# The seam between attention and the output projections: last gate products placed between its steps, last head split from PSUM, five heads' outputs loaded into the places of E

## The chip, the cores and the metric

The kernel runs on one core of a Trainium2 chip. The metric is the device time of one execution in microseconds (us). Before the change it is 1768.91 us, the median of three runs (1768.19, 1768.91 and 1770.76).

A core has engines that run side by side, each through its own list of instructions in its own order. PE multiplies matrices, DVE and ACT do elementwise work, POOL here mostly clears small tiles, and SP issues nearly all DMA transfers. They meet through semaphores: an instruction waits until another engine, or a transfer, has counted far enough. While it waits, everything behind it on its engine waits too.

## The reference, cut to what matters

One layer of a decoder, on 1024 tokens of width 1024. The change concerns the end of the attention branch and the start of its projection:

```python
h = rms_norm(x, attn_norm_w)
q, k, v, u, g = split(h @ w_in)                 # g: 2048 columns, 16 blocks of 128
p = softmax(q1 k1 * scale + bias) - lam * softmax(q2 k2 * scale + bias)   # causal, 8 heads
a = rms_norm(p @ v, subln_w) * (1 - lam_init)   # per head, 128 wide
y_a = a.reshape(S, 1024) @ w_proj_attn
c = silu(layer_norm(causal_conv(u_a * sigmoid(u_b)), conv_ln_w, conv_ln_b))
y_b = c @ w_proj_conv
g_a, g_b = split(sigmoid(g + gate_b))
x = x + (g_a * y_a + g_b * y_b) @ w_out
x = x + swiglu(rms_norm(x, ffn_norm_w))
```

## The kernel before, in words

Every float32 product is made of three: both operands are split into a high part (a cast on ACT, `split_hi`, line 120) and a remainder (a subtraction on DVE, `split_lo`, line 125), and `mm3` (lines 152 to 155) adds high times high, high times low and low times high in one PSUM bank. A block of 512 tokens by 128 columns over the 1024 inputs is `gemm_T`: 8 steps of 3, so 24 products of 128x512.

The weights come through a stream, `ws`, that loads two blocks ahead. Its split tiles (`whi`, `wlo`) have three places, so the cast of a later block waits until the products of the block three places before it are done.

The gates. For each of 16 column blocks c, `g_item(c)` makes two halves (`G0` to `G15` below): 24 products into a bank `pg`, a copy with bias on ACT into `sgg`, a store to DRAM in `g_d`. While attention runs, a list `later` holds these and the Q items as filling between attention steps; `plan` says how many pieces each head gets. The last entry of `later`, `["G14", "G15"]`, belongs to no head.

Attention. A loop goes over 8 heads h times 8 blocks i of 128 queries. `scores(h, i)` makes the scores of both softmax halves in banks `sc`; DVE adds the bias and finds the minimum into tiles `E` (four places); ACT takes the exponential (line 1059); DVE joins the two halves (lines 1065 to 1069). In the loop's next turn `turn(h, i)` transposes the joined E on PE (`pT`, line 1088) and splits it into `ph` and `pl`. For each pair of blocks, `weigh(h, b)` multiplies with V (`pW`, 24 products of 128x256 for the last pair), `back` transposes the result (`pB`) and scales it into `an`, `subln` normalises the head, and `subln_T` transposes it (`pS`), scales it into `at` and stores it to DRAM in `a_d`. Everything outside the products that a head needs is put between pieces of G or Q products by hand: `after(ins)` makes what is written in its block stand behind `ins` on its engine.

After the loop (lines 1210 to 1226), the kernel turns, weighs and normalises the last pair of the last head, while the products of G14 and G15 stand behind its `weigh`. Then the pools of attention close, and the tiles `aT_hi` and `aT_lo` of all 8 heads are made from loads of `a_d` in halves of 512 tokens, 16 loads of 256 KB (`early` for heads 0 to 3, `at` for 4 to 7), each followed by its two splits. The first two column blocks of the projection run with the head k as the outer loop, so that they can start on the first head alone (lines 1344 to 1351). The layer norm of the convolution (`ln_chunks`) is spread between the projection's column blocks. PE meets it in its own list at two products `mean`, two `pm` and two `rstd`, and DVE makes the sums for them (`lns`) between other work. A tile scheduler orders what the code leaves open, by its own estimates.

## Time and profile before

| | us |
|---|---|
| runs without the profiler, median of 3 | 1768.91 (1768.19 to 1770.76) |
| the profiled execution, its own time | 1769.82 |
| its span, first to last instruction | 1768.0 |
| PE busy in the span | 1740.1 (98%) |
| DVE busy | 1273.1 (72%) |
| ACT busy | 800.8 (45%) |
| mean granted PE clock | 0.997 |

A profile shows one execution. Times in its views are us from the start of the span. A row of the timeline gives start, busy time, engine, line, operation, out<-in, shape and count; a bracket at its end is idle time of that engine before the row, and what ended it. Busy times of products overlap, since a product's end runs beside the next one's start: the distance between two starts is what a product costs PE. The end of attention lies between 815 and 852 us, and the projection of the heads begins at 851.31.

### The profile page before, as it was taken

The page shows a single profiled execution, that of the slowest core. Times are in us where ns is not written, and L with a number is a line of the kernel's source. Part 1 is how long each engine was busy: PE and PEld are TensorE (multiplying, and loading weights), DVE is VectorE, ACT ScalarE, POOL GpSimd, SP SyncE. Part 2 cuts the span into 40 slices and gives each one's busy share as a digit, 9 for nine tenths or more (in the row PEclk, how much of TensorE's full clock was granted, in tenths as well). Part 3 has the DMA queues.
Part 4 walks back from the last instruction along what each step waited for, and adds up shares of the span by engine and source line. Part 5 has one row for each costly group of instructions (what it writes and reads, how often), then busy time and mean ns, then how long its engine had stood idle before and what let it go on. Part 6 is the DMA issues. An engine that isn't in the chain of part 4 may idle for free.

```text
span 1768.0 us, 25005 instructions
## 1 busy us (share of the span) xinstructions
PE 1740.1 (98%) x8983; PEld 1484.6 (84%) x8983; DVE 1273.1 (72%) x2171; ACT 800.8 (45%) x1883; POOL 19.6 (1%) x92
## 2 busy tenths in 40 slices
PE   6999999999999999999999999999999999999999
PEld 5778898998999998987788888878888888888887
DVE  6598888998898888885677534867667666665544
ACT  5221141557767776754457313633333333333332
POOL 0000000000000000000000000000000000000000
PEclk9999999999999999999999999999999999999999
DMA  6337334235443244341973544224544544697663
GB/s 231 107 125 232 131 111 115 70 104 138 120 141 105 82 125 145 97 147 60 339 261 108 167 166 143 90 90 152 171 159 148 177 153 148 202 357 250 214 214 131
DMA packets 251110, 275.29 MB, mean 156 GB/s; under 512 B 16505, under 2 KB 166050, under 8 KB 250986
## 3 DMA queue, kind: packets, MB, share of 16 engines
q1 hardware_dynamic: 249130, 267.47, 47.0%
q0 software_dynamic: 1280, 4.91, 0.9%
q10 hardware_dynamic: 576, 1.31, 0.3%
q8 instruction: 71, 1.16, 0.3%
q14 instruction: 53, 0.43, 0.1%
HBM read 176.59 MB, written 78.68 MB: 144 GB/s over the span
## 4 chain that ended last, share of the span: by engine, by line
PE 91%; DMA 3%; DVE 2%; ACT 2%; issue 1%; SPq 0%; DVEq 0%; ACTq 0%
PE acc L1611 19%; PE pg L153 14%; PE pg L154 14%; PE pg L155 14%; PE acc L497 12%; PE pg L688 4%; PE sc L1053 2%; PE sc L1052 2%; PE pT L1088 2%; PE wo L154 2%; PE wo L153 2%; PE wo L155 2%; PE pW L155 1%; PE pW L153 1%; PE pW L154 1%
## 5 line engine op out<-in xcount | busy, mean ns | idle before, releaser
L569 DVE SCALAR_TENSOR_TENSOR acc<-u,cw,acc 128x1024 f32<-128x1024 f32 x240 | 306.9, 1279 | 2.9
L153 PE MATMUL pg<-hT_hi,whi 128*128 128x512 f32 x512 | 201.7, 394 | 0.5 <-ACT hT_hi L120 0.2
L154 PE MATMUL pg<-hT_lo,whi 128*128 128x512 f32 x512 | 200.9, 392 | 0.0
L155 PE MATMUL pg<-hT_hi,wlo 128*128 128x512 f32 x512 | 200.7, 392 | 0.0
L120 ACT CAST whi<-wraw 128x1024 fp32r<-128x1024 f32 x101 | 106.1, 1051 | 182.9 <-PE pg L154 99.5
L125 DVE TENSOR_TENSOR wlo<-wraw,whi 128x1024 fp32r<-128x1024 f32 x101 | 123.0, 1219 | 63.3 <-ACT whi L120 59.4
L125 DVE TENSOR_TENSOR wlo<-draw,whi 128x1024 fp32r<-128x1024 f32 x75 | 91.8, 1224 | 89.1 <-ACT whi L120 86.1
L153 PE MATMUL pg<-whi,hT_hi 128*128 128x256 f32 x512 | 146.0, 285 | 0.3 <-ACT jk L756 0.3
L155 PE MATMUL pg<-whi,hT_lo 128*128 128x256 f32 x512 | 145.8, 285 | 0.0
L154 PE MATMUL pg<-wlo,hT_hi 128*128 128x256 f32 x512 | 145.5, 284 | 0.0
L120 ACT CAST whi<-draw 128x1024 fp32r<-128x1024 f32 x75 | 79.1, 1055 | 129.5 <-PE acc L497 122.6
L1059 ACT ACTIVATE E<-E,mn 128x256 f32<-128x256 f32 (+7 forms) x128 | 99.6, 780 | 45.9 <-DVE mn L1054 44.7
L497 PE MATMUL acc<-wlo,whi 128*128 128x512 f32 x308 | 119.8, 389 | 0.0
L497 PE MATMUL acc<-whi,wlo 128*128 128x512 f32 x308 | 119.8, 389 | 0.0
L153 PEld LDWEIGHTS pg<-hT_hi,whi 128*128 128x128 f32 x512 | 96.2, 188 | 20.5 <-ACT sgg L603 0.7
L155 PEld LDWEIGHTS pg<-hT_hi,wlo 128*128 128x128 f32 x512 | 96.2, 188 | 19.1
L154 PEld LDWEIGHTS pg<-hT_lo,whi 128*128 128x128 f32 x512 | 96.2, 188 | 19.0 <-issue 0.6
L153 PEld LDWEIGHTS pg<-whi,hT_hi 128*128 128x128 f32 x512 | 97.7, 191 | 2.2 <-ACT jk L756 1.0
L154 PEld LDWEIGHTS pg<-wlo,hT_hi 128*128 128x128 f32 x512 | 97.7, 191 | 1.3
L155 PEld LDWEIGHTS pg<-whi,hT_lo 128*128 128x128 f32 x512 | 97.7, 191 | 0.4
L1611 PE MATMUL acc<-h_hi,whi 128*128 128x512 f32 x240 | 93.4, 389 | 0.0
L1611 PE MATMUL acc<-h_lo,whi 128*128 128x512 f32 x240 | 93.4, 389 | 0.0
(280 smaller groups left out, 4191.1 us busy)
## 6 DMA issues: line engine op xcount, KB each, us to landing
wraw<-in_w_gate_up_dram SPq DMA_DIRECT2D x44, 512.0 KB, 4.8
wraw<-in_w_in_dram SPq DMA_DIRECT2D x38, 512.0 KB, 4.2
qs<-qs SPq DMA_DIRECT2D x96, 128.0 KB, 2.3
wd<-in_w_down_dram SPq DMA_DIRECT2D x44, 256.0 KB, 3.2
tdT<-wd SPq DMA_DIRECT2D x88, 128.0 KB, 4.5
draw<-sdS SPq DMA_DIRECT2D x44, 256.0 KB, 2.6
draw<-tdT SPq DMA_DIRECT2D x44, 256.0 KB, 4.3
wraw<-in_w_in_dram SPq DMA_DIRECT2D x32, 256.0 KB, 3.4
```

Source lines behind the costliest of these rows:

```text
L120: act.copy(dst, src)
L125: last_lo[0] = dve.tensor_tensor(dst, src, f32(hi), op=ALU.subtract).ins
L153: pe.matmul(o, lh, rh, start=start, stop=False)
L154: pe.matmul(o, lh, rl, start=False, stop=False)
L155: last_mm[0] = pe.matmul(o, ll, rh, start=False, stop=stop).ins
L497: m = pe.matmul(o[s_][i][:], l_[:, ts], r_[:, 512:], start=start and j + y_ == 0, stop=j == n - 1 and y_ == 2, skip_group_check=not start,)
L569: dve.scalar_tensor_tensor(acc[0][:], us[c][:, t : t + S], cw[:, c, t : t + 1], acc[0][:], op0=ALU.mult, op1=ALU.add)
L688: last_mm[0] = pe.matmul(o[:], l_, r_, start=first and n_ == 0, stop=last and n_ == len(terms) - 1).ins
L1052: pe.matmul(o[:, :w], qh[:, qs], k, start=True, stop=False)
L1053: last_mm[0] = pe.matmul(o[:, :w], ql[:, qs], k, start=False, stop=True).ins
L1059: act.activation(e[:, :nk], e[:, :nk], AF.Exp, bias=mn[:, j : j + 1], scale=-1.0, accum_out=l[:, j : j + 1])
L1611: pe.matmul(o[:], a_[x_][:, k, :], b_[y_][:, k, :], start=start and k + x_ + y_ == 0, stop=k == 3 and x_ == 1, skip_group_check=not start,)
```

## The change

The list of fillings is run without its last entry, and the work after the loop is written anew:

- The pools of the convolution and of Q and K close right after the loop, and tiles `aTh` and `aTl` of six heads (`KA` = 0, 1, 2, 3, 4, 7) are opened in their place.
- G14's first half (`g_half(14, 0)`) stands right behind the loop, on PE ahead of the last `turn`. Then come `turn`, a `back`, and `weigh` of the last pair. The second half of G14 follows, with the last `back` in its middle, then the two halves of G15.
- Heads 0 to 4 are loaded from `a_d` in one piece each (512 KB) into the four places of `E` and into the place of the bias tile `tb`, and split whole (128x1024). The loads of heads 5 and 6 stay in halves, behind the closing of the attention pools.
- The last head is no longer stored and loaded: its `pS` is scaled and cast by ACT into `aTh` and its remainder is taken by DVE, both straight from PSUM.
- The first two column blocks of the projection take the heads in the order 0, 1, 2, 3, 4, 7, 5, 6.

```diff
+    def g_half(c, sb, w, amid=None):
+        o = gemm_T(w, hT_hi, hT_lo, sb, amid)
+        sg = wp.tile([P, 512], F32, tag="sg", name=nm("sgg"), bufs=2)
+        act.activation(sg[:], o[:], AF.Identity, bias=pcol("gate_b", c))
+        nc.sync.dma_start(g_d[c][:, sb * 512 : (sb + 1) * 512], sg[:])
...
-    fill = run(it for l_ in later for it in l_)
+    fill = run(it for l_ in later[:-1] for it in l_)
...
-    n = len(steps)
-    turn(*steps[-1])
-    weighs.append((n, steps[-1][:1] + (NT // 2 - 1,)))
-    slot(n, len(late))
-    m = last_mm[0]
-    while backs or sublns:
-        n += 1
-        slot(n, 0)
-    with after(m):
-        for _ in fill:
-            bg.step(2)
+    bg.until(0)
+    qk_ctx.close()
+    cv_ctx.close()
+    yp_ctx = ExitStack()
+    ypa = yp_ctx.enter_context(tc.tile_pool(name="ypa", bufs=1, side="right", reuse_waits="tile"))
+    KA = (0, 1, 2, 3, 4, NKT - 1)
...
+    aT_hi, aT_lo = y_tiles("aT", KA)
...
+    hl, bl = H - 1, NT // 2 - 1
+    with behind(E_.PE, E_.Activation, E_.DVE):
+        wg = ws.next()
+        g_half(14, 0, wg)
+    with after(last_mm[0]):
+        turn(*steps[-1])
+        for h, b, ar in ready(backs, len(steps)):
+            back(h, b, ar)
+        ar = weigh(hl, bl)
+    early = {}
+    for h in KA[:-1]:
+        early[h] = aps.tile([P, S], F32, tag="E" if h < 4 else "tb", name=f"early{h}", bufs=4 if h < 4 else 1)
+        nc.sync.dma_start(early[h][:], a_d[h][:])
+    with after(last_mm[0]):
+        g_half(14, 1, wg, lambda: back(hl, bl, ar))
+    subln(hl)
+    with behind(E_.Activation, E_.DVE):
+        for h in KA[:-1]:
+            split_hi(aT_hi[h][:], early[h][:])
+            split_lo(aT_lo[h][:], early[h][:], aT_hi[h][:])
+    wg = ws.next()
+    with after(last_mm[0]):
+        g_half(15, 0, wg)
+    with after(last_mm[0]):
+        for sb in range(2):
+            cs = slice(sb * 512, (sb + 1) * 512)
+            pt = pm("pS")
+            for i in range(4):
+                pe.transpose(pt[:, i * P : (i + 1) * P], AN[hl][:, 4 * sb + i, :], ident[:])
+            hi = aT_hi[hl][:, cs]
+            act.activation(hi, pt[:], AF.Identity, scale=pcol("subln"))
+            dve.scalar_tensor_tensor(
+                aT_lo[hl][:, cs], pt[:], pcol("subln"), f32(hi), op0=ALU.mult, op1=ALU.subtract
+            )
+        g_half(15, 1, wg)
...
-    for k in range(NKT):
+    for n, k in enumerate(KA + KB):
...
```

The first place is on PE, at the end of the loop. `pT<-ident,E` are the transposes of `turn`, of block 6 of the last head in the first two rows and of block 7 (`E_9102`) after; `pB` and `pW` belong to `back` and `weigh`. Before:

```order
L1088 MATMUL pT_9159<-ident,E_9000 128x128 x4
L1088 MATMUL pT_9166<-ident,E_9000 128x128 x3
L1088 MATMUL pT_9172<-ident,E_9102 128x128 x4
L1088 MATMUL pT_9179<-ident,E_9102 128x128 x4
L1108 MATMUL pB_9186<-ident,ar_9098 128x128 x2
L153 MATMUL pW_9194<-ph_9155,vh_8604 128x256
```

After it, the first and the last rows of the part that is new, with the rows around it (`pg_9195` is the bank of G14's first half):

```order
L1091 MATMUL pT_9166<-ident,E_9000 128x128 x3
L153 MATMUL pg_9195<-hT_hi,whi_8859 128x512
L154 MATMUL pg_9195<-hT_lo,whi_8859 128x512
L155 MATMUL pg_9195<-hT_hi,wlo_8860 128x512
...
L1091 MATMUL pT_9223<-ident,E_9102 128x128 x4
L1091 MATMUL pT_9230<-ident,E_9102 128x128 x4
L1111 MATMUL pB_9237<-ident,ar_9098 128x128 x2
L153 MATMUL pW_9245<-ph_9155,vh_8604 128x256
```

The 24 products of G14's first half now stand between the transposes of block 6 and those of block 7; `pT`, `pB` and `pW` of the last pair still follow one another.

The second place is on ACT, at the same point of the program. `E<-E,mn` is the exponential, `whi<-wraw` the cast of a weight block, `sgg<-pg` the copy of a gate half, `ph<-pT` the cast of the transposed E. Before:

```order
L1059 ACTIVATE E_9102,l_9101<-E_9102,mn_9100 128x1024
L1102 COPY ar_9098<-pW_9079 128x256
L120 CAST whi_9258<-wraw_9256 128x1024
L1059 ACTIVATE E_9112,l_9101<-E_9112,mn_9100 128x1024
L603 ACTIVATE sgg_9152<-pg_9127,pvec 128x512
L120 CAST ph_9155<-pT_9159 128x4x128
L120 CAST ph_9155<-pT_9166 128x3x128
L120 CAST ph_9155<-pT_9172 128x4x128
L120 CAST ph_9155<-pT_9179 128x4x128
```

And after the change:

```order
L1062 ACTIVATE E_9102,l_9101<-E_9102,mn_9100 128x1024
L1105 COPY ar_9098<-pW_9079 128x256
L1062 ACTIVATE E_9112,l_9101<-E_9112,mn_9100 128x1024
L601 ACTIVATE sgg_9152<-pg_9127,pvec 128x512
L120 CAST ph_9155<-pT_9159 128x4x128
L120 CAST ph_9155<-pT_9166 128x3x128
L120 CAST whi_9191<-wraw_9189 128x1024
L601 ACTIVATE sgg_9220<-pg_9195,pvec 128x512
L120 CAST ph_9155<-pT_9223 128x4x128
L120 CAST ph_9155<-pT_9230 128x4x128
```

The cast of the weight block moves from ahead of the last exponential to behind the casts of block 6, and the copy of G14's first half (`sgg_9220`) now stands ahead of the casts of block 7.

The third place is in SP's list of transfers, between the last store of the convolution (`c_d_132`) and the loads of the layer norm (`cT_lo<-c_d`). Before, ten rows from the store of G15's first half on:

```order
L604 DMA g_d_148<-sgg_9349 128x512
L1248 DMA early_0_9406<-a_d_109 128x512
L1248 DMA early_1_9410<-a_d_109 128x512
L1248 DMA early_0_9414<-a_d_110 128x512
L1248 DMA early_1_9418<-a_d_110 128x512
L1248 DMA early_0_9422<-a_d_111 128x512
L1248 DMA early_1_9426<-a_d_111 128x512
L1248 DMA early_0_9430<-a_d_112 128x512
L1248 DMA early_1_9434<-a_d_112 128x512
L1248 DMA at_0_9438<-a_d_113 128x512
```

After the change, from the store `c_d_132` on:

```order
L573 DMA c_d_132<-acc_7505 128x1024
L1252 DMA early_9272<-a_d_109 128x1024
L1252 DMA early_9280<-a_d_113 128x1024
L1252 DMA early_9274<-a_d_110 128x1024
L602 DMA g_d_146<-sgg_9152 128x512
L1252 DMA early_9276<-a_d_111 128x1024
L298 DMA wraw_9471<-in_w_proj_attn_dram 128x8x128
L602 DMA g_d_147<-sgg_9220 128x512
L1252 DMA early_9278<-a_d_112 128x1024
L602 DMA g_d_147<-sgg_9315 128x512
L298 DMA wraw_9477<-in_w_proj_attn_dram 128x8x128
L602 DMA g_d_148<-sgg_9370 128x512
```

The loads of heads 0 to 4 stand ahead of the stores of G14 and G15 now, where before all 16 halves stood behind the store of G15's first half.

More of the change, by code (lines that the diff above doesn't have):

```diff
@@ L366, in kt @@
     def kt(m, k):
[L367 removed]
+        return m[k] if isinstance(m, dict) else m[:, k, :]
     def gemm_T(w, mhi, mlo, sb, amid=None):
@@ L600, in g_item @@
         for sb in range(2):
-            o = gemm_T(w, hT_hi, hT_lo, sb)
-            sg = wp.tile([P, 512], F32, tag="sg", name=nm("sgg"), bufs=2)
-            act.activation(sg[:], o[:], AF.Identity, bias=pcol("gate_b", c))
-            nc.sync.dma_start(g_d[c][:, sb * 512 : (sb + 1) * 512], sg[:])
+            g_half(c, sb, w)
             yield
@@ L1209 @@
         due -= int(due + 1e-6)
-    n = len(steps)
-    turn(*steps[-1])
-    weighs.append((n, steps[-1][:1] + (NT // 2 - 1,)))
-    slot(n, len(late))
-    m = last_mm[0]
-    while backs or sublns:
-        n += 1
-        slot(n, 0)
-    with after(m):
-        for _ in fill:
-            bg.step(2)
-    inatt[0] = False
+    assert next(fill, None) is None and not late
     bg.until(0)
-    del pms[1:]
-    at_ctx.close()
     qk_ctx.close()
@@ new lines, with behind @@
+    E_ = mybir.EngineType
+    def behind(*engines):
+        st = ExitStack()
+        for e_ in engines:
+            st.enter_context(after(last_of(e_)))
+        return st
+    hl, bl = H - 1, NT // 2 - 1
[7 more added lines that the diff above has]
+        ar = weigh(hl, bl)
+    assert not backs and not weighs and not sublns
@@ L1241 @@
-    for h in range(H):
+    KB = tuple(k for k in range(NKT) if k not in KA)
+    for d_, more_ in zip((aT_hi, aT_lo), y_tiles("aT", KB)):
+        d_.update(more_)
+    for h in KB:
         for sb in range(2):
             cs = slice(sb * 512, (sb + 1) * 512)
-            if h < 4:
-                at = bp.tile([P, 512], F32, tag=("s", "sq", "z", "csg")[h], name=f"early{h}_{sb}", bufs=2)[:]
-            else:
-                at = bp.tile([P, 512], F32, tag="ya", name=f"at{h}_{sb}", bufs=4)[:]
+            at = bp.tile([P, 512], F32, tag="ya", name=f"at{h}_{sb}", bufs=4)[:]
```

24 lines of the change are left out of this document (14 added, 10 removed).

## The prediction

> **What bounds the kernel now.** I read the page first (span, slices, the chain), then PE's timeline at the end of attention, then the other engines there, then the stages after it.
>
> ```profile
> span 1768.0 us, 25005 instructions
> ...
> PE   6999999999999999999999999999999999999999
> ...
> PE 91%; DMA 3%; DVE 2%; ACT 2%; issue 1%; SPq 0%; DVEq 0%; ACTq 0%
> ```
>
> PE is the bound: 91% of the chain that ended last is PE's own work. A change pays only where PE waits or runs slowly. PE's timeline has four kinds of rows at the seam that tell how much of this there is:
>
> ```profile
> 815.66 0.92 PE L1088 MATMUL pT<-ident,E 128*128 128x128 f32 x7
> 819.74 1.94 PE L1088 MATMUL pT<-ident,E 128*128 128x128 f32 x8 [3.15 <-DVE E L1068]
> 821.47 0.63 PE L1108 MATMUL pB<-ident,ar 128*128 128x128 f32 x2
> 822.22 0.58 PE L153 MATMUL pW<-ph,vh 128*128 128x256 f32 x1
> ...
> 826.55 0.28 PE L153 MATMUL pW<-ph,vh 128*128 128x256 f32 x1
> ...
> 826.91 0.39 PE L153 MATMUL pg<-hT_hi,whi 128*128 128x512 f32 x1
> ...
> 849.64 0.39 PE L155 MATMUL pg<-hT_hi,wlo 128*128 128x512 f32 x1
> 851.31 1.09 PE L153 MATMUL pg<-aTh,whi 128*128 128x512 f32 x3 [1.28 <-ACT aTh L120]
> ```
>
> The brackets show two waits: 3.15 us for the last joined E, and 1.28 us for the first head's cast. Between them something else is slow: from 819.74 to 826.91 PE needs 7.17 us for 8 transposes, 2 more and 24 `pW`. The windows tell why (columns: stretch, length, then busy time of PE, PEld, DVE, ACT, POOL, the granted clock, DMA share, GB/s):
>
> ```profile
> 820.00:822.00 2.00, 2.00 (x10) 1.70 (x8) 1.18 (x3) 0.87 (x2) 0.20 (x1) 0.50 0.82 271
> ...
> 824.00:826.00 2.00, 2.00 (x11) 2.00 (x11) 0.00 (x0) 0.00 (x0) 0.00 (x0) 0.50 0.00 0
> 826.00:828.00 2.00, 2.00 (x14) 1.83 (x13) 0.00 (x0) 0.37 (x1) 0.00 (x0) 0.96 0.00 0
> ```
>
> The granted clock is 0.50 from 820 until about 826: the long wait is followed by a stretch at half speed.
>
> **The sum.** First what the work costs at full clock. A transpose is 0.11 us (the `pS` row below, 8 in 0.88). A `pW` is 0.12 (826.55 to 826.91 is three of them). A gate product: from 826.91 to 849.64 lie 95 steps, 2 `pB` and 8 `pS`, so (22.73 - 10 x 0.11) / 95 = 0.2277 us.
>
> ```profile
> 841.63 0.88 PE pS L1129 x8
> ```
>
> From 815.66 to 851.31 are 35.65 us. The work in it: 27 transposes (15 `pT`, 4 `pB`, 8 `pS`) 2.97, 24 `pW` 2.88, 96 gate products 21.86, together 27.71. So 7.94 us are lost: 3.15 and 1.28 in the two waits, 7.17 - 3.98 = 3.19 in the slow stretch (3.98 is 10 transposes and 24 `pW`), and 0.3 in hops. The change makes the same products, so only these 7.94 us, and what it adds, are at stake.
>
> **Part 1: G14's first half ahead of the last transposes.** It is 24 x 0.2277 = 5.46 us of work that needs nothing from the last head. PE starts it at 815.66 + 0.77 = 816.43 and ends its issue at 821.89. The joined E is there earlier than that:
>
> ```profile
> 815.63 1.05 ACT L120 CAST whi<-wraw 128x1024 fp32r<-128x1024 f32 x1 [0.79 <-PE pg L154]
> 816.58 1.15 ACT L1059 ACTIVATE E<-E,mn 128x1024 f32<-128x1024 f32 x1
> ...
> 820.86 0.59 ACT L120 CAST ph<-pT 128x512 fp32r<-128x512 f32 x1 [1.62 <-PE pT L1088]
> ...
> 816.71 1.23 DVE L125 TENSOR_TENSOR wlo<-wraw,whi 128x1024 fp32r<-128x1024 f32 x1 [1.01 <-ACT whi L120]
> ...
> 818.30 1.28 DVE L1068 SCALAR_TENSOR_TENSOR E<-E,rl,E 128x1024 f32<-128x1024 f32 x1
> ...
> 821.48 0.69 DVE L125 TENSOR_TENSOR pl<-pT,ph 128x512 fp32r<-128x512 f32 x1 [0.82 <-ACT ph L120]
> ```
>
> Even in the old order E is complete at 819.58; now the weight cast (1.05) no longer stands ahead of the exponential, so about 818.7. The 3.15 us are covered with 3 us to spare, and with them goes what I take for the cause of the half clock, another 3.19. If the cover failed, both would come back.
>
> **What is late next.** `pT` and `pB` of the last pair take 1.10 us (821.89 to 822.99), then `pW` needs the first four blocks of `ph` and `pl`. In ACT's new order the copy of G14's first half stands ahead of those casts. A gate product's row is 0.39 long and the last starts at 821.66, so the copy starts near 822.1. Copy 0.69 (row below), cast 0.59, subtraction 0.69 follow one another, so `pW` starts at 824.1: a **new wait of 1.1 us**. Bounds: 0.8, had ACT taken the cast right behind the first four transposes; 1.4, what lay there before (822.22 - 819.74 - 1.10, at half clock).
>
> ```profile
> L603 ACT ACTIVATE sgg<-pg,pvec 128x512 f32<-128x512 f32 x4 | 2.8, 688 | 1.3 <-PE pg L155 1.3
> ```
>
> From there PE is fed: `pW` 2.88, G14's second half with `pB` 5.69 (the copy `ar` has 21 products of time), G15 and `pS` 11.81. The projection starts at 824.1 + 20.4 = **844.5 instead of 851.3**.
>
> **Part 2: heads 0 to 4 in E's places.** Before, their first load is asked for at 845.76 and PE waits for it:
>
> ```profile
> 845.76 4.12 SPq L1248 DMA_DIRECT2D early<-a_d  x8
> ...
> early<-a_d SPq DMA_DIRECT2D x8, 256.0 KB, 5.4
> ...
> 834.06 0.17 DVE L646 TENSOR_SCALAR v<-ssa 128x8 f32<-128x8 f32 x1 [11.04 <-ACT jk L1117]
> ...
> 835.56 1.22 DVE L1122 TENSOR_TENSOR an<-an,r 128x1024 f32<-128x1024 f32 x1
> ```
>
> Now the last of the five is asked for when E's last transpose is done, near 823, and ACT casts them behind the norm of the last head. G14 ends at 832.7; a weight cast (1.05), the copy (0.69) and a square (0.6) stand on ACT, then 2.72 us of small steps and `an` (834.06 to 836.78): `an` at 837.8. Transfers of 256 KB landed in 5.4 us with the queues full; twice the size has 12 us here. Costs: ACT 5 x 1.05 = 5.3, DVE 5 x 1.22 = 6.1 (the 128x1024 rows above), so DVE is done at 843.9. The projection needs head 0 at 844.5 (ready 839.0) and head 4 only 13 products later, at 847.5. G15 hides all this; without that cover DVE's 6.1 would be on the path. So the 1.28 goes, and 0.25 with it that the first three products lose after it (851.31 to 852.24 for 0.68).
>
> **Part 3: the last head from PSUM.** The store, two loads and their landing disappear. ACT scales and casts at once, as `at<-pS` did. The remainder from PSUM with a scale is not in this place before; its nearest row is the same form for K:
>
> ```profile
> L781 DVE SCALAR_TENSOR_TENSOR klo<-pQ,pvec,ks x3: 743/744/750, 703.1 to 768.5; 128x512 fp32r<-128x512 f32 x3
> ```
>
> Two of 0.74 behind 843.9 end at 845.4; the first product that waits for them is the 17th, at 848.1. Nothing on the path; at twice the price, 846.9, still nothing. Heads 5 and 6 are asked for behind the first `cT_lo` load, which waits for the last product on hT_lo (844.3), and are needed 72 products later, at 860.9.
>
> **Total.** 35.65 + 0.25 before, 27.71 + 1.1 after (0.1 of hops in it): 7.0 to 7.1 us less. Against the profiled execution 1769.82 - 7.05 = 1762.8. The median was 0.9 below that execution; the half-clock stretch that I remove may vary from run to run and be part of this, so I carry only half of it: **1762.4**. Behind 851 PE has no wait over 0.15 us until 1176, so a shift there reaches the end, unless PE meets something that has not moved with it.
>
> **The rule of the skill.** The clock first in rows: besides the stretch above, one other wait is followed by 0.50, and one is not.
>
> ```profile
> 1176.58 0.50 PE L1611 MATMUL acc<-T2h,whi 128*128 128x512 f32 x1 [2.42 <-ACT whi L120]
> ...
> 1178.00:1180.00 2.00, 2.00 (x5) 1.63 (x6) 1.22 (x1) 0.96 (x1) 0.00 (x0) 0.50 0.82 228
> ...
> 850.00:852.00 2.00, 0.72 (x4) 0.40 (x3) 0.71 (x2) 1.32 (x3) 0.00 (x0) 1.00 0.93 332
> ```
>
> So 2.42 us were enough once, 1.28 were not. The Trainium skill, "TensorE: Matmul & The Clock Gate", section "Why this matters for your kernels", puts the bound at gaps over about 3 us; the row at 1178 speaks against so late a bound. Its section "Part 4: PE-mode transpose" adds that transposes don't count as busy PE in the same way. By the first rule the new wait of 1.1 us costs no clock; by the second, 1.1 us of transposes and 1.1 of wait lie together.
>
> **Rivals.** (a) *The clock still drops.* Transposes and the new wait make 2.2 us without dense products, near the 2.42 that sufficed. One stretch like that at 1178 (about 3.4 us at half speed) costs 1.7: 1764.1. Against it: 1.28 did not suffice, and busy transposes are not idle. 12%.
>
> (b) *The layer norm gets in the way.* PE's list meets the second `pm` 276 rows behind the projection's start, where it was 305: 29 x 0.2277 = 6.6 us earlier, relative to that start. Before:
>
> ```profile
> 860.00:870.00 10.00, 10.00 (x44) 7.93 (x43) 7.93 (x13) 4.28 (x8) 0.00 (x0) 1.00 1.05 405
> ...
> 920.19 0.69 DVE L1280 TENSOR_TENSOR lns<-lns,lnsq 128x512 f32<-128x512 f32 x1 [2.24 <-ACT lnsq L1277]
> ...
> 923.26 0.79 PE pm L1286 x8
> ...
> L120 ACT CAST aTh<-early 128x512 fp32r<-128x512 f32 x8 | 4.5, 618 | 5.4 <-DMA early<-a_d 5.3
> ```
>
> DVE's sum ended at 920.88, 2.4 us ahead of PE. If the norm's work keeps its distance to the start, PE waits 6.6 - 2.4 = 4.2: 1766.6. Against it: 12 subtractions of half heads leave DVE's full stretch there (12 x 0.6 = 7.2 us), and 12 casts of 0.62 leave ACT's. 13%, some of it smaller.
>
> (c) *Slower: the layer norm does not move at all.* The DMA share is 1.05 at 860 to 870; were the norm bound by transfers, its sum would still end at 920.9, while PE comes to the second `pm` at 844.5 + 276 x 0.2277 = 907.3. The wait is 13.6, the time 1762.4 + 13.6 = 1776.0. It decides from 914.4 on, where the wait eats the 7. Against it: its first load waits for the last product on hT_lo, which moves, and 10 of the 16 halves now load at 816 to 828. 6%.
>
> (d) *The filling doesn't fill.* G14's first half waits for its bank or weights, and the old wait stays under another name, with the slow stretch, and only the end's 1.28 + 0.25 are gained: 1769.8 - 1.5 = 1768.3. The weights were split long before, and the bank's last copy was of G13's first half. 7%.
>
> **How the numbers follow.** Forecast 62%, within 1760.2 to 1764.6: the low end is 1762.8 less the 0.9 and less 1.7, should the slow stretch at 1178 fall away by chance; the high end adds the wait's bound and small waits. The range goes up to (b), 1760.2 to 1766.6. A measurement of this kernel can tell about 0.2%, 3.5 us, from no change. Faster by more: the forecast, (a) and the small part of (b), 78%. Within: the rest of (b), and (d), 15%. Slower 7%.
>
> **What would show it.** In the new profile: no bracket at the transposes of block 7; a clock of 1.00 through 816 to 845; a bracket near 1 us at the first `pW`; the first `aTh` product near 844.5 with no bracket; no bracket at `mean`, `pm` or `rstd`. A new wait at any of the last three, or 0.50 behind `pW`, makes the prediction wrong by the prices above.

## The result, and the profile after

| | before | changed |
|---|---|---|
| runs beside each other, median | 1770.8 us (6 runs, 1768.19 to 1772.96) | 1764.17 us (6 runs, 1761.77 to 1765.22) |
| ratio | | 0.9964, 95% interval 0.9953 to 0.9976 |
| the profiled execution and its span | 1769.82, 1768.0 | 1765.22, 1763.4 |

The changed kernel is faster by 0.36% (0.24% to 0.47%), 6.4 us of 1770.8 by that ratio. The forecast was 1762.4 within 1760.2 to 1766.6. The page of the changed kernel, its span and the shares of the chain that ended last:

```profile
span 1763.4 us, 24974 instructions
...
PE 90%; DMA 3%; DVE 3%; ACT 2%; issue 1%; SPq 0%; ACTq 0%; DVEq 0%
```

PE still bounds the kernel. PE's timeline at the seam, in the order of the rows shown before:

```profile
816.21 0.92 PE L1091 MATMUL pT<-ident,E 128*128 128x128 f32 x7
...
822.46 1.04 PE L1091 MATMUL pT<-ident,E 128*128 128x128 f32 x8
823.34 0.38 PE L1111 MATMUL pB<-ident,ar 128*128 128x128 f32 x2
824.61 0.39 PE L153 MATMUL pW<-ph,vh 128*128 128x256 f32 x1 [0.89 <-DVE pl L125]
...
845.08 0.39 PE L153 MATMUL pg<-aTh,whi 128*128 128x512 f32 x1
```

The bracket of 3.15 at the transposes of block 7 is gone, and eight of them take 1.04 instead of 1.94. The first product on `aTh` has no bracket. One new bracket stands at the first `pW`. The windows (stretch, length, busy time of PE, PEld, DVE, ACT and POOL, granted clock, DMA share, GB/s) where the clock stood at 0.50 before:

```profile
820.00:822.00 2.00, 2.00 (x10) 1.66 (x9) 1.49 (x2) 0.00 (x0) 0.00 (x0) 1.00 0.95 337
...
824.00:826.00 2.00, 1.39 (x11) 1.40 (x12) 1.15 (x2) 1.55 (x7) 0.00 (x0) 1.00 1.14 334
```

From the first transposes of block 6 to the first `aTh` product there were 35.65 us before; now there are 845.08 - 816.21 = 28.87. So the seam is 6.78 shorter, but the span of this execution only 4.6. PE's waits in the stage behind the seam, 850 to 1000 us (engine, line, what it waited for, us, times, longest), have two new rows:

```profile
PE pg L153 <- ACT cT_hi L120: 0.9, 1, 0.9
PE rstd L1336 <- DVE lnz L1339: 0.7, 1, 0.7
```

Both are waits for the layer norm.

### The profile page after: what moved, and what is told of

Read it like the earlier page. It is cut to its first block, busy times and chain, and to the rows that moved or that the text cites. A ratio compares the mean times of both kernels' runs of the same rounds, so it can differ in the third digit from the quotient of the medians.

```text
span 1763.4 us, 24974 instructions
## 1 busy us (share of the span) xinstructions
PE 1737.2 (99%) x8983; PEld 1481.3 (84%) x8983; DVE 1272.2 (72%) x2166; ACT 799.0 (45%) x1876; POOL 19.6 (1%) x92
## 4 chain that ended last, share of the span: by engine, by line
PE 90%; DMA 3%; DVE 3%; ACT 2%; issue 1%; SPq 0%; ACTq 0%; DVEq 0%
PE acc L1656 21%; PE pg L153 12%; PE pg L154 12%; PE pg L155 12%; PE acc L497 12%; PE pg L691 4%; PE sc L1056 2%; PE sc L1055 2%; PE pT L1091 2%; PE wo L153 2%; PE wo L155 2%; PE wo L154 2%; DMA ya_d<-gt 1%; PE pW L155 1%; DMA gt<-g_d 1%
```

## How the runs are compared

Single executions of one kernel differ by 2.6 to 6.3 us, once by 8.6, and most of the edits below are worth 1 to 7. What repeats far better is the length of a stage in the profiles, between two rows of PE's timeline. The marks are the starts of: the transposes of block 6 (`pT`, x7), the first product on `aTh`, the first on `cT_hi`, the first on `wo`, and the first on `T2h` in the feed-forward. Each number is the difference of two such starts; the first and the last column are what lies ahead of block 6 and behind `T2h`. All in us:

| kernel | ahead | seam | aTh to cT_hi | cT_hi to wo | wo to T2h | behind | span |
|---|---|---|---|---|---|---|---|
| before | 815.66 | 35.65 | 92.01 | 87.04 | 146.22 | 591.42 | 1768.0 |
| changed | 816.21 | 28.87 | 93.07 | 88.44 | 146.22 | 590.59 | 1763.4 |
| changed, again | 815.40 | 28.87 | 93.04 | 87.04 | 146.25 | 590.20 | 1760.8 |
| filler only | 817.98 | 38.06 | 94.59 | 87.04 | 146.20 | 591.43 | 1775.3 |
| filler only, loads first | 816.11 | 31.05 | 94.97 | 87.04 | 146.22 | 592.01 | 1767.4 |
| no filler | 816.00 | 33.96 | 91.73 | 87.04 | 146.22 | 590.05 | 1765.0 |
| short filler | 816.39 | 30.54 | 91.72 | 87.03 | 146.25 | 589.07 | 1761.0 |
| late loads | 814.89 | 29.02 | 92.45 | 87.04 | 146.22 | 589.78 | 1759.4 |
| last head by store | 815.46 | 28.86 | 93.00 | 87.04 | 146.20 | 590.04 | 1760.6 |
| turn inside the filler | 816.29 | 27.82 | 92.12 | 87.03 | 146.23 | 591.01 | 1760.5 |
| five gate tiles | 815.39 | 28.86 | 92.62 | 90.01 | 146.30 | 590.32 | 1763.5 |
| gates behind the norm | 816.11 | 28.87 | 91.95 | 87.04 | 146.21 | 590.62 | 1760.8 |
| turn inside, gates behind | 814.33 | 27.82 | 92.52 | 87.04 | 146.27 | 590.62 | 1758.6 |

What is to be seen: the seam of the changed kernel is 28.86 or 28.87 in five profiles, its own two and those of three kernels whose edits leave PE's seam as it is. The stage ahead (814.3 to 818.0) and the stage behind (589.1 to 592.0) differ by up to 3.7 us without any edit that reaches them. That is the noise of single executions, and a verdict below rests on the stage that an edit touches. Part of the noise goes with the clock. Every profile has the wait of 2.42 us at the first product on `T2h`; in 7 of the 13 a stretch at granted clock 0.50 follows it, in 6 it does not (below), and the last column averages 591.0 with that stretch and 590.0 without.

## The experiments

### The parts one by one

The change has three parts: the filler (G14's first half ahead of the last turn), the early loads (heads 0 to 4 into E's places), and the last head straight from PSUM. First the filler alone, with nothing else of the change:

```diff
-    with behind(E_.Activation, E_.DVE):
-        for h in KA[:-1]:
-            split_hi(aT_hi[h][:], early[h][:])
...
-            hi = aT_hi[hl][:, cs]
-            act.activation(hi, pt[:], AF.Identity, scale=pcol("subln"))
+        subln_T(hl)
...
-    for h in KB:
+    for h in range(H):
```

> Only the filler of the change is kept: the first half of gate product 14 stands ahead of the last turn (and the second half and product 15 behind it, as in the change). Heads 0 to 4 are loaded again into the layer norm's buffers behind the attention, the last head goes through its store and load, and the output products run in the order of the heads. Theory of the prediction (the filler alone takes away the 3.15 us wait and the half-clock stretch; the loads alone take away 1.28 + 0.25): no bracket of 3 us at the transposes of block 7, granted clock 1.00 through the seam, and the waits of 1.28 and 0.25 us on the splits at the first output products are back. The time stands about 1.5 us above the changed kernel: 1765.7 against 1764.2. Rival (what the loads gain at the seam is given back in the layer norm, because the layer norm does not get earlier by as much as the products do): the two waits that the changed kernel has in the layer norm (0.74 us ahead of the rstd transposes, 0.85 us at the first product on cT_hi) shrink here by about as much as the start of the output products is later, and the time is that of the changed kernel within 0.4 us.

Measured: 1776.39 us (5 runs, 1774.43 to 1777.04) beside 1769.63 before; ratio 1.0038, interval 1.0025 to 1.005. Both theories missed: the filler alone makes the kernel slower. PE's row at the first `aTh` product:

```profile
856.04 1.22 PE L153 MATMUL pg<-aTh,whi 128*128 128x512 f32 x2 [9.04 <-ACT aTh L120]
```

The wait is not 1.28 but 9.04 us. The old wait at block 7 did go (the seam has no other bracket than 0.89 at `pW`), so the filler did its work there and uncovered something else. SP's timeline of this run shows it:

```profile
846.40 0.32 SPq L1135 DMA_DIRECT2D a_d<-at  x1
846.81 0.38 SPq L1289 DMA_DIRECT2D cT_lo<-c_d  x1
...
848.78 0.38 SPq L602 DMA_DIRECT2D g_d<-sgg  x1
849.20 0.43 SPq L1289 DMA_DIRECT2D cT_lo<-c_d  x1
849.67 5.35 SPq L1271 DMA_DIRECT2D early<-a_d  x8
```

The loads of heads 0 to 3 leave at 849.67, behind the last head's store, four loads of the layer norm and the last gate store. Before, they left at 845.76, and G15 ran on for 4 us more. Here PE has nothing left from 847.0 on, 2.7 us ahead of them. The products moved ahead of the last turn had covered this round trip.

Then the late loads and the last head by store, each one part undone from the changed kernel:

```diff
-    KA = (0, 1, 2, 3, 4, NKT - 1)
+    KA = (NKT - 1,)
...
-    early = {}
-    for h in KA[:-1]:
-        early[h] = aps.tile([P, S], F32, tag="E" if h < 4 else "tb", ...)
-        nc.sync.dma_start(early[h][:], a_d[h][:])
```

> The changed kernel without the early loads: heads 0 to 4 are loaded behind the attention into the layer norm's buffers, as before; the filler stays ahead of the last turn, the last head goes straight from PSUM and is the first that the output products take. Theory, after the run with the filler alone (the part of gate products 14 and 15 that is moved ahead of the last turn used to cover the round trip of heads 0 to 4; with it gone from there, the loads stand behind the last gate store in SP's queue and PE waits for them): the 12 products on the last head cover 2.7 of the 9.0 us, so a wait of about 6.3 us stands behind them, with a half-clock stretch behind it, and the time is 1771 to 1774 us. Rival (the 9.0 us came from the last head's store and load, not from heads 0 to 4): no wait over 1.5 us, 1764 to 1766.

Measured: 1763.59 us (5 runs, 1761.32 to 1766.86) beside 1769.21 before; ratio 0.9965, interval 0.9953 to 0.9977. The theory missed, and the rival held in its waits: none at the heads, a seam of 29.02 (the time is 0.4 us under its range). SP's timeline tells what differs from the run with the filler alone:

```profile
838.34 0.32 SPq L602 DMA_DIRECT2D g_d<-sgg  x1
838.75 2.79 SPq L1287 DMA_DIRECT2D early<-a_d  x6
845.41 0.32 SPq L602 DMA_DIRECT2D g_d<-sgg  x1
```

Six of the same eight loads into the same kind of buffers leave from 838.75 on, 11 us earlier (7.8 us earlier counted from the transposes of block 6). The last head's store is gone from SP's list, and the scheduler put them ahead of the last gate store. That the missing store is the reason was not tested apart from the other differences of the two runs.

```diff
-            hi = aT_hi[hl][:, cs]
-            act.activation(hi, pt[:], AF.Identity, scale=pcol("subln"))
-            dve.scalar_tensor_tensor(
-                aT_lo[hl][:, cs], pt[:], pcol("subln"), f32(hi), op0=ALU.mult, op1=ALU.subtract
-            )
+        subln_T(hl)
```

> The changed kernel with the last head's outputs stored and loaded again, as before, instead of split straight from PSUM; the filler stays ahead of the last turn and heads 0 to 4 still come early into E's places; heads 5, 6 and 7 are loaded behind the attention. Theory of the prediction (the straight split is worth nothing on the path, since five heads' products, 13.6 us, stand ahead of it): no wait of PE at the first products on aTh nor between the heads, and the time is the changed kernel's within 0.4 us, 1763 to 1764.5. Rival, after the run with the filler alone (the last head's store stands in SP's queue ahead of loads that are needed soon): heads 5 and 6 come late, PE waits 1 us or more between the heads, and the time is over 1765.

Measured: 1763.27 us (6 runs, 1761.85 to 1767.38) beside 1769.53; ratio 0.997, interval 0.9958 to 0.9981; seam 28.86, no wait between the heads. As the theory said. So with the filler, either of the two other parts is enough, and the second adds nothing that shows.

The cause was still argued from the order of issues, with several things changed at once. The next run changes only the issues in the kernel with the filler alone: the last head's two stores go by ACT's queue, and the loads stand ahead of the last gate store and of the layer norm's loads (`ld3` is the last load of head 3; each `add_manual_dep` orders two transfers within SP's list):

```diff
-            nc.sync.dma_start(a_d[h][:, sb * 512 : (sb + 1) * 512], at[:])
+            (nc.scalar if h == H - 1 else nc.sync).dma_start(a_d[h][:, sb * 512 : (sb + 1) * 512], at[:])
...
-            nc.sync.dma_start(cc[c], c_d[c][:, cs])
+            cl_ = nc.sync.dma_start(cc[c], c_d[c][:, cs]).ins
+            tc.add_manual_dep(cl_, ld3.name, ...)
...
+    tc.add_manual_dep(g_last, ld3.name, ...)
```

> The run with the filler alone, with nothing changed but the order of DMA issues: the last head's two stores go out by ACT's queue instead of SP's, and SP issues the loads of heads 0 to 4 ahead of the last gate store and of the loads of the layer norm's inputs (which wait for the last gate product to free their place). Theory (the 9.0 us wait and the slow clock behind it came from the order in SP's queue: the loads stood behind the last head's store, the first load into the layer norm's place and the last gate store): the loads are issued at about 842 instead of 849.7 us, PE's wait at the first product on aTh falls from 9.0 to under 1.5 us, and the time from 1776.4 to 1764 to 1766. Rival (the loads wait for the memory of the attention's tiles, or the round trip itself is too long): the wait stays over 4 us and the time over 1769.

Measured: 1769.44 us (11 runs, 1766.13 to 1771.7) beside 1769.53; ratio 1.0, interval 0.9991 to 1.0009. From the timelines of SP, ACT and PE:

```profile
839.97 9.51 SPq L1271 DMA_DIRECT2D early<-a_d  x8
...
845.92 0.69 ACT L601 ACTIVATE sgg<-pg,pvec 128x512 f32<-128x512 f32 x1
846.50 2.17 ACT L120 CAST aTh<-early 128x512 fp32r<-128x512 f32 x4
...
847.16 1.66 PE L153 MATMUL pg<-aTh,whi 128*128 128x512 f32 x4 [2.03 <-ACT aTh L120]
```

The issues alone take 7.0 of the 9.0 us (seam 38.06 to 31.05): it was the queue. But the expected 1764 to 1766 is missed by 3 to 5 us. The data are there now; the casts of head 0 stand behind the last head's scaling, a weight cast and the last gate copy in ACT's list and begin at 846.50, while PE is done at 845.1. A half-clock stretch follows the 2.03 us wait (below), and the stage up to `cT_hi` is 94.97, 1.9 more than in the changed kernel. In the changed kernel the five casts are done by 841.3, so PE finds heads 0 to 4 split.

### Without the filler

```diff
+    wg = ws.next()
     with behind(E_.PE, E_.Activation, E_.DVE):
-        wg = ws.next()
-        g_half(14, 0, wg)
-    with after(last_mm[0]):
         turn(*steps[-1])
...
+    with after(last_mm[0]):
+        g_half(14, 0, wg)
     with after(last_mm[0]):
         g_half(14, 1, wg, lambda: back(hl, bl, ar))
```

> All of the change but the filler: both halves of gate product 14 stand behind the last weighing. Theory of the prediction: the wait at the transposes of block 7 is back at 2.3 to 3.2 us, and the half-clock stretch of 3.4 us behind it too (3.2 us of PE time), so that only the 1.5 us at the first output products are gained: 1769.3 us against 1770.8 before and 1764.2 of the change. Rival (the half-clock stretch was not due to this wait, or a wait shorter than 3 us does not bring it): the wait is there and the granted clock stays at 1.00: 1766.1 us. Second rival (the layer norm limits the time as soon as the loads are early): the 1.5 us do not show in the time, 1770.8.

Measured: 1766.75 us (11 runs, 1764.67 to 1768.7) beside 1769.63; ratio 0.9986, interval 0.9977 to 0.9995. PE, ACT and DVE at the seam:

```profile
820.08 1.94 PE L1091 MATMUL pT<-ident,E 128*128 128x128 f32 x8 [3.15 <-DVE E L1071]
...
815.97 1.05 ACT L120 CAST whi<-wraw 128x1024 fp32r<-128x1024 f32 x1 [0.79 <-PE pg L154]
816.92 1.15 ACT L1062 ACTIVATE E<-E,mn 128x1024 f32<-128x1024 f32 x1
...
818.64 1.28 DVE L1071 SCALAR_TENSOR_TENSOR E<-E,rl,E 128x1024 f32<-128x1024 f32 x1
```

and the windows behind the wait:

```profile
820.00:822.00 2.00, 1.92 (x9) 1.95 (x10) 1.18 (x3) 0.59 (x1) 0.00 (x0) 0.50 0.72 232
824.00:826.00 2.00, 2.00 (x12) 2.00 (x11) 0.00 (x0) 0.00 (x0) 0.00 (x0) 0.54 0.89 365
826.00:828.00 2.00, 2.00 (x15) 1.83 (x14) 0.00 (x0) 0.37 (x1) 0.00 (x0) 1.00 0.04 16
```

The theory held in mechanism: wait and half clock are both back, unchanged. The seam is 33.96, 1.69 shorter than before, and the stage behind it 0.28 shorter; 1.28 and 0.25 were expected. The run keeps both the early loads and the last head from PSUM, so it does not tell these two apart. The seam is 5.09 longer than in the changed kernel: that is what the filler is worth once the loads are out of the way. The median lies 2.9 us under before where 1.5 was expected; the interval (0.9 to 4.1 us) holds both.

### How long the filler must be

```diff
-        g_half(14, 0, wg)
+        og = pg()
+        g_ks(og, range(0, 2))
     with after(last_mm[0]):
         turn(*steps[-1])
...
+    with after(last_mm[0]):
+        g_ks(og, range(2, 8))
```

Each step of `g_ks` is 3 products.

> The changed kernel with only 6 of the 24 products of the first half of gate product 14 ahead of the last turn; the other 18 and their copy stand behind the weighing. 6 products take 1.36 us of the 3.15 us, so a wait of about 1.8 us is left at the transposes of block 7. Theory (the granted clock falls with any such wait that is long against its window of 3.4 us; 2.4 us were enough further down in this kernel): a half-clock stretch of 3.4 us follows the 1.8 us wait, and the seam is 1.8 + 3.2 less 0.9 us longer than the changed kernel's, 4 us in all: 1767 to 1768. Rival (1.8 us is too short for it): the granted clock stays at 1.00, the seam is 1 to 2 us longer, 1764.5 to 1765.5.

Measured: 1765.56 us (9 runs, 1762.98 to 1768.58) beside 1769.53; ratio 0.9979, interval 0.9969 to 0.9988. PE's rows and the windows around them:

```profile
816.39 0.93 PE L1091 MATMUL pT<-ident,E 128*128 128x128 f32 x7
...
819.63 1.17 PE L1091 MATMUL pT<-ident,E 128*128 128x128 f32 x8 [0.92 <-DVE E L1071]
820.63 0.41 PE L1111 MATMUL pB<-ident,ar 128*128 128x128 f32 x2
822.33 0.39 PE L153 MATMUL pW<-ph,vh 128*128 128x256 f32 x1 [1.30 <-DVE pl L125]
```

```profile
818.00:820.00 2.00, 1.08 (x8) 0.63 (x6) 1.97 (x4) 2.00 (x4) 0.00 (x0) 1.00 1.14 309
820.00:822.00 2.00, 1.04 (x9) 0.64 (x7) 2.00 (x4) 1.79 (x7) 0.00 (x0) 1.00 0.85 337
```

The seam is 30.54, 1.67 longer than the changed kernel's, so the rival held in size. But the question on a wait of 1.8 us stays open: the wait came out at 0.92, since the weight cast moved behind the exponential here as in the changed kernel, and E was joined earlier. What the run does show: two waits of 0.92 and 1.30, with only 1.4 us of transposes between them, left the clock at 1.00 in this execution.

### The new wait at the weighing

```diff
-        g_half(14, 0, wg)
+        og = pg()
+        g_ks(og, range(0, 4))
     with after(last_mm[0]):
         turn(*steps[-1])
+    with behind(E_.PE, E_.Activation):
+        g_ks(og, range(4, 8))
...
+    with after(last_mm[0]):
         for h, b, ar in ready(backs, len(steps)):
```

> The changed kernel with the last turn put in the middle of the filler: 12 products of gate product 14, then block 7's transposes, then the other 12 products and their copy, then the weighing. Theory (the 0.89 us wait at the first weighing product comes from the copies ph and pl standing behind the copy of the gate product, with nothing left on PE to cover them): that wait goes, the seam from the first transposes of block 6 to the first product on aTh takes 28.0 us instead of 28.87, and the time is 0.9 us less than the changed kernel's, 1763.3. Rival (the layer norm behind the seam sets the end of the stage, so an earlier seam is waited out there): the wait goes, the two waits in the layer norm (0.74 and 0.85 us) grow by 0.9 together, and the time stays at 1764.2. Third: 12 products are too short to cover block 7's softmax chain, and a wait of about 2.8 us less 2 times 2.6 stands at the transposes instead: nothing gained.

Measured: 1762.52 us (5 runs, 1761.51 to 1764.1) beside 1769.63; ratio 0.9963, interval 0.9951 to 0.9975. PE's rows:

```profile
816.29 0.93 PE L1091 MATMUL pT<-ident,E 128*128 128x128 f32 x7
...
819.83 1.04 PE L1091 MATMUL pT<-ident,E 128*128 128x128 f32 x8
823.47 0.38 PE L1111 MATMUL pB<-ident,ar 128*128 128x128 f32 x2
823.61 0.36 PE L153 MATMUL pW<-ph,vh 128*128 128x256 f32 x1
```

No bracket is left: 12 products cover E's chain, the other 12 cover the casts and subtractions `ph` and `pl`. The seam is 27.82, 1.05 shorter than the changed kernel's (0.9 expected). So the wait at `pW` came from a copy and a split with nothing beside them on PE. In the time the step does not show above the noise: 0.9963 beside 0.9964.

### What the layer norm takes back

> The changed kernel itself once more, so that it stands on the same chip beside the runs sent with it. Theory (its time hangs on how late the layer norm's casts are, and these hang on how long single stores and loads of the gate tiles take): 0.9964 of before again, 1763 to 1765 us, with single executions spread over 3 us or more; its profile shows waits of 0.5 to 2.5 us in all at the first products on cT_hi and the rstd transposes, not the same ones in the same sizes. Rival (these two waits are fixed): 0.74 and 0.85 us again.

Measured: 1763.41 us (5 runs, 1762.57 to 1767.03) beside 1769.21; ratio 0.9968, interval 0.9956 to 0.998. The time and the spread came as the theory said, and PE's waits from 850 to 1000 us are not the same ones. But it placed them at `cT_hi` and `rstd`, and there it missed.

```profile
PE pg L153 <- DVE gt L1383: 1.0, 1, 1.0
```

Neither `rstd` nor `cT_hi` waits in this execution; the first projection's banks wait 1.02 us for DVE at 868.12 instead. The last cast to `cT_hi` begins at 959.84 in the first execution and at 956.04 in the second. Part of the reason is in SP's and ACT's timelines. Here the first execution, the one with the wait:

```profile
942.73 0.32 SPq L1384 DMA_DIRECT2D ya_d<-gt  x1
945.61 0.32 SPq L1375 DMA_DIRECT2D gt<-g_d  x1
...
948.40 0.63 ACT L1376 ACTIVATE gt<-gt 128x512 f32<-128x512 f32 x1 [2.03 <-DMA gt<-g_d]
948.94 0.81 ACT L1340 ACTIVATE lnz<-lnz,pvec 128x512 f32<-128x512 f32 x1
...
955.25 0.64 ACT L1376 ACTIVATE gt<-gt 128x512 f32<-128x512 f32 x1 [1.63 <-DMA gt<-g_d]
```

A gate tile is free for the next load only when its last use is stored to `ya_d`. The sigmoids `gt` of the second projection's fourth and fifth gates stand in ACT's list ahead of the layer norm's last two pairs of chunks (`lnz`, then the casts), and wait for their loads. In the second execution the same two sigmoids begin at 944.69 and 951.47, 3.7 and 3.8 us earlier, while PE's first `cT_hi` product is only 0.84 us earlier. But 3.0 of the 3.8 us are there already at a cast ahead of both (938.51 beside 935.48). The lag grew before, from 0.5 us at the sigmoid of 892.02 to 3.2 at that of 919.57, which waited 2.81 us for its load where its counterpart waited 1.70. So these two sigmoids are the end of the chain and not the whole of it, and that the time of single stores and loads decides whether PE notices is read from these rows; no run tests it.

Two tries at this chain. One gate tile more:

```diff
-        g = bp.tile([P, 512], F32, tag="gt", name=nm("gt"), bufs=4)
+        g = bp.tile([P, 512], F32, tag="gt", name=nm("gt"), bufs=5)
```

> The changed kernel with five gate tiles gt instead of four, so that a gate load waits for the store of ya_d of the fifth last use, not of the fourth last. Theory (the layer norm is late because its casts stand in ACT's queue behind sigmoids that wait for gate loads, and those for stores): ACT's waits on gate loads between 846 and 970 us fall from 49 us in all to under 40, the two waits of 0.74 and 0.85 us at the layer norm shrink, and the time is 0.8 to 2.0 us less than the changed kernel's: 1762.2 to 1763.4. Rival (the layer norm is late because of its own chain of sums on DVE and squares on ACT, whose start did not move by as much as the products did): the waits on gate loads change, the two waits on PE stay at 0.7 to 0.9 us, and the time stays within 0.3 us of 1764.2.

Measured: 1766.73 us (11 runs, 1762.62 to 1771.23) beside 1769.63; ratio 0.9986, interval 0.9977 to 0.9996. A miss, and rather slower than the changed kernel: the stage from `cT_hi` to `wo` is 90.01, with a wait of 2.5 us for `cT_hi`. A fifth tile does not make ACT wait less for gates (26.5 us from 846 to 965 beside 26.0 in the changed kernel's first profile; the 49 us that the expectation starts from are not found there). The run refutes the number of tiles as the remedy, not the queue as the cause; what made it slower was not followed further.

The other try leaves the tiles and moves the two sigmoids behind the layer norm's last cast:

```diff
-        act.activation(g[:], g[:], AF.Sigmoid)
+        sig = act.activation(g[:], g[:], AF.Sigmoid).ins
+        if ins is not None:
+            tc.add_manual_dep(sig, ins.name, ...)
...
-                g = gated(g_d[NKT + c], cs)
+                g = gated(g_d[NKT + c], cs, ln_end[0] if sb else None)
```

> The changed kernel with two instructions of ACT placed elsewhere: the sigmoids of the fourth and fifth gate of the second projection (needed by the products of its second half only) stand behind the layer norm's last cast instead of ahead of its last two pairs of chunks. Theory (ACT waits there for gate loads that wait for a store or for a product, with the layer norm's last casts behind them in its queue): the two idle stretches of ACT ahead of these sigmoids (2.03 and 1.63 us in the changed kernel's profile) no longer stand ahead of a layer norm cast, the last cast to cT_hi ends some 3.5 us earlier, the wait of 0.85 us and the 0.56 us of slow spacing at the first product on it are gone, and the time is 1.0 to 1.4 us less than the changed kernel's in the same batch, with a smaller spread. The wait of 0.74 us at the rstd transposes stays, since the gates ahead of it are not moved. Rival (the casts are late from DVE's side): the wait stays at 0.5 us or more, and the time within 0.4 us of the changed kernel's.

Measured: 1763.36 us (7 runs, 1761.05 to 1767.39) beside 1769.21; ratio 0.9968, interval 0.9957 to 0.998. ACT's timeline at the end of the layer norm:

```profile
952.90 0.61 ACT L120 CAST cT_hi<-lnz 128x512 fp32r<-128x512 f32 x1
953.82 0.62 ACT L120 CAST cT_hi<-lnz 128x512 fp32r<-128x512 f32 x1 [0.32 <-DVE lnz L1344]
954.35 1.15 ACT L1379 ACTIVATE gt<-gt 128x512 f32<-128x512 f32 x2
```

The last cast begins at 953.82, 6 us ahead of the changed kernel's first profile (959.84) and 2.2 ahead of its second (956.04). This profile has no PE wait at all from 850 to 1000; the one at `rstd`, which was expected to stay, is absent too. The stages behind the seam are 91.95 and 87.04, together the shortest with the whole filler. In the medians nothing shows: 1763.36 beside 1763.41 in the same batch, and the spread is not smaller. So the expected 1.0 to 1.4 us is missed. That the edit brings the cast forward is shown; that it takes a wait from PE is not, since the second profile without the edit has none at `cT_hi` either.

> Both edits together on the changed kernel: the last turn in the middle of the filler, and the two sigmoids behind the layer norm. Theory: the 0.89 us wait at the weighing and the 0.85 us wait at cT_hi are both gone; 1.0 us less than the kernel with the two sigmoids moved alone, about 2.2 us less than the changed kernel, 1761 to 1762. Rival (what is gained ahead of the layer norm is waited out in it): the time of the kernel with the sigmoids moved alone, within 0.4 us.

Measured: 1763.42 us (5 runs, 1760.35 to 1765.0) beside 1769.21; ratio 0.9962, interval 0.995 to 0.9974. The expected 1761 to 1762 is missed, and the rival's number came: the time is that of the kernel with the sigmoids moved alone. In the profile, however, the seam is 27.82 again and the two norm waits are absent. It has the shortest span of all profiles, 1758.6, but 1.88 of the 4.8 us to the changed kernel's first profile lie ahead of the edits. In the seam and the two stages behind it this version is 1.6 us shorter than the changed kernel's second profile and 3.0 than its first; by the times the three versions are not told apart.

## Why the prediction was right, point by point

**What bounds, and the sum.** Held. What changed on PE beyond the noise lay in the seam and in the two stages behind it. The forecast seam was 844.5 - 815.66 = 28.84 us; 28.87 was measured, twice.

**Part 1, the filler.** Held: no bracket at block 7 and a clock of 1.00 throughout; in the run without the filler the 3.15 us wait and the half clock are back. Also the smaller step held, that E is complete about 0.85 us earlier because the weight cast no longer stands ahead of the exponential: in the changed kernel DVE joins E from 818.01 with block 6 at 816.21, 1.80 behind it; without the filler from 818.64 with 816.00, 2.64 behind it.

**What is late next.** A wait of 1.1 at `pW` was forecast, within 0.8 to 1.4, by copy, cast and subtraction in a row; 0.89 was measured, by this chain. ACT's and DVE's rows of the changed kernel:

```profile
822.66 0.69 ACT L601 ACTIVATE sgg<-pg,pvec 128x512 f32<-128x512 f32 x1 [2.76 <-PE pg L155]
823.25 1.06 ACT L120 CAST ph<-pT 128x512 fp32r<-128x512 f32 x2
...
823.86 1.29 DVE L125 TENSOR_TENSOR pl<-pT,ph 128x512 fp32r<-128x512 f32 x2 [2.37 <-ACT ph L120]
```

The chain ended as forecast: `pW` starts 8.40 us behind the transposes of block 6, where 8.44 was forecast. The bracket is shorter because PE's last rows ahead of it, the two `pB`, end at 823.72, 1.26 us behind the start of block 7's transposes and not 1.10. The turn inside the filler shows that the wait belongs to this place.

**Part 2, the early loads.** The term was right in the sum, and its reason was too narrow. The prediction priced the loads at 1.28 + 0.25, the wait that was there before. The wait goes, and in the run without the filler, where parts 2 and 3 stand together, 1.69 of the seam and 0.28 behind it go. But the price holds only while the filler stands behind the weighing: with the filler moved ahead and the loads left where they were, 9.04 us stand there. The prediction treated the parts as a sum, and they are not one.

**Part 3, the last head from PSUM.** Held as priced: undone alone it costs nothing. What the prediction did not see is that it would also have carried the change in place of part 2: with it and late loads the seam is 29.02.

**Total.** 7.05 was forecast for the profiled execution. The seam gave 6.78, and the layer norm and the projections took back 1.06 and 1.40 in the first profiled execution, 1.03 and 0 in the second. The step that was off is the sentence that a shift there reaches the end: rival (b), the layer norm in the way, came in part, with 2.46 us in the first execution, at `rstd` and `cT_hi` and not at `pm`; in the second a wait for DVE at the projection's banks took 1.03. Neither reached its 4.2. By the prediction's own sign, a bracket at `mean`, `pm` or `rstd`, the 0.74 at `rstd` marks this step as wrong.

The time fits better than these two executions, and part of that is luck. The medians gave 6.6 and 5.8 us, and the forecast was 6.5 below 1768.91; but seam and stages behind it gave only 4.3 and 5.75. The measured 1764.17 lies 1.8 above the forecast's 1762.4 mainly because the kernel before, run beside it, took 1770.8 and not 1768.91. The chance that the low end of the range names, that the slow stretch at `T2h` falls away, came in the changed kernel's second profile and not in its first.

**The rivals.** (a) did not come: the 0.89 us wait left the clock at 1.00. (c) and (d) did not come. A slower case was there all the same, though not the one written down: the filler without either of the other parts.

**The rule.** The Trainium skill, "TensorE: Matmul & The Clock Gate", section "Why this matters for your kernels", says that gaps over about 3 us bring the half clock. The new wait of 0.89 agrees with it; the 2.03 us of the run with the loads first speaks against so late a bound, as 2.42 did before; but 2.42 was followed by the half clock in only 7 of the 13 profiles.

## What to carry to other kernels

Work that fills one wait is often the cover of another. Before moving it, look at what its old place hid, transfers above all, and at what stands ahead of those in the issuing engine's list. A part that is worth nothing when undone alone may be what makes another part pay, so test parts both alone and left out. And where single executions differ by more than the effect, compare stage lengths between fixed rows of the bounding engine.

## What the runs showed of the hardware

A wait of 2.03 us was followed by the half clock. The windows of the run with the loads first, behind the wait that ends at 847.16:

```profile
847.00:849.00 2.00, 1.84 (x5) 1.38 (x6) 2.00 (x5) 1.66 (x4) 0.00 (x0) 0.70 0.43 166
849.00:851.00 2.00, 2.00 (x6) 1.57 (x5) 1.82 (x4) 1.14 (x2) 0.00 (x0) 0.50 0.67 195
```

But the length of a wait alone does not decide. The wait of 2.42 us at the first product on `T2h` is the same in all 13 profiles. In 7 of them, the one before the change among them, the clock falls to 0.50 behind it; in 6 it stays at 1.00. Here the changed kernel's second profile, and then the wait at `cT_hi` in the run with five gate tiles, which also leaves the clock at 1.00:

```profile
1170.60 0.50 PE L1656 MATMUL acc<-T2h,whi 128*128 128x512 f32 x1 [2.42 <-ACT whi L120]
...
1172.00:1174.00 2.00, 2.00 (x9) 1.66 (x10) 1.41 (x2) 1.07 (x2) 0.00 (x0) 1.00 0.80 222
...
959.90 0.73 PE L153 MATMUL pg<-cT_hi,whi 128*128 128x512 f32 x2 [2.47 <-ACT cT_hi L120]
...
962.00:964.00 2.00, 2.00 (x10) 1.65 (x10) 1.12 (x2) 1.14 (x2) 0.00 (x0) 1.00 0.19 26
```

The wait of 3.15 was followed by 0.50 in both profiles that have it, and the one of 9.04 in its one. Between 815 and 1000 us single waits of up to 1.30 us never were, nor were 0.92 and 1.30 with 1.4 us of transposes between them. In the opening of the kernel, where waits and transposes lie close together, six waits of 1.70 to 2.13 us near 17 us were each followed by 0.50 and seven of 1.49 were not, while one of 2.2 near 28 us met it in one profile of 13. So a wait of 2.2 to 2.4 us costs a half-clock stretch in one execution and nothing in the next, and these runs show no one bound. The Trainium skill, "TensorE: Matmul & The Clock Gate", section "Part 1: The HAM clock gate (the "warmup" mystery)", says that the clock is decided over free-running windows of about 3.4 us. That would fit a wait that is sometimes followed by the half clock and sometimes not; no run here shows the windows themselves.
